# Two-layer hybrid trunk on one core: homes for a layer's first weights, order of the end-of-layer squares, stream order of the last product, queue of the solve's loads

## The chip, the cores and the metric

The kernel runs on one core of one Trainium2 chip. The core's engines work from queues of their own and meet through semaphores: TensorE (PE; its weight loads PEld), VectorE (DVE), ScalarE (ACT), GpSimd (POOL) and SyncE (SP), and DMA queues that ACT, POOL and SP issue. The metric is the device time of one execution in microseconds (us); lower is better.

## The reference, cut to what matters

```python
for l in range(2):                                  # DEPTH; x is (1, 256, 2048), float32
    h = rmsnorm(x, norm_pre[l])                     # x * rsqrt(mean(x*x) + 1e-6) * gain
    pa, pb, pc, pd, pm = split(h @ w_in[l])         # four mixers' columns and the merge gates
    ys = [gla(pa), sparse_attention(pb), rwkv7(pc), spatial_gating(pd)]   # each (256, 1024)
    merged = sum(sigmoid(pm[g]) * (ys[g] @ w_proj[l, g]) for g in range(4))
    x = x + rmsnorm(merged @ w_out[l], norm_post[l])
```

The rwkv7 mixer is a recurrence in time; the kernel computes it in chunks, for which small triangular systems are solved. All matrix products are to be right to float32.

## The kernel before, in words

**Weights as one stream.** The 256 tokens are two halves of 128, t = 0 and 1. All large weights lie in one DRAM tensor `w`, packed by the host in the order in which they are used. `weights()` (L187) reads it on SyncE's queue: one DMA brings four k-steps (128 rows of the contraction each) into a `raw` tile, 1 MB where a product is 512 wide; there are three such tiles (RAW_BUFS = 3). Each k-step is split into a high part `wh` (ACT, L154) and a rest `wl` (DVE, L157), and six matmuls follow, three for each half of the tokens (`tok_mm`, L169). `wh` and `wl` have three buffers each, so the splits run at most three k-steps ahead of TensorE. Steps named in `apart` get tiles of their own (`wown`), which wait for none of the three; for steps named in `alone`, the three matmuls of t = 0 come first, and those of t = 1 only after the last such step.

**Order.** The framework lays the program out on a timeline that it works out when the kernel is built, with priorities; after that each engine executes its own list in that fixed order. A wait on an engine holds all that stands behind it in the list.

**A layer.** `pre` transposes the normalised tokens (`trT`, L173) and evicts each block twice: a high part on ACT, the rest on DVE (`xT`). `small` (L455) is the first product, 280 wide, with nine steps in `wown`, in tiles of class `c8`. Eight products `c_pair` follow (tile `mc` on TensorE), then `c_solve` (L628), then the other mixers, the merges and `finish`.

**The solve.** During the c_pairs, POOL writes factors to DRAM (`Gd`). `c_solve` reads them back in another layout: eight loads of 64 KB into `slv` (L637) and four into `TT` (L657), all issued by ACT's queue, while TensorE runs the next product. DVE then works through the substitution (`slvt`, `slv`).

**The end of a layer.** `finish` (L1010) runs four products d = 0..3 with `w_out`. For each and each half, ACT squares the result (`junk`, with a sum) and DVE scales it into `o`. The last, d = 3, keeps steps 8..15 in `wown` (also class `c8`, four buffers) and has 5..15 in `alone`: t = 0 is complete before t = 1's long stretch. Then come the sum of squares (`orsq`, whose power is on POOL), `x <- o*orsq + x` (L1040) in four quarters per half, the write of x to DRAM (`xs`, L1041, POOL's queue) and, in layer 0, the norm of the next layer: four Squares on ACT, the sum and power (`ss`, POOL L183), and the scaled result, again in `o`, two quarters on DVE and two on ACT. At the start of the program the norm of each half takes two quarters by `bn_stats` on DVE and two by Squares on ACT.

Of the kernel before, what the change touches and what calls it, by code (L numbers as in the profile page):

```python
# [30 lines left out]
RAW_BUFS, SPLIT_BUFS = 3, 3  # L31

# [46 lines left out]
def pack_stream(w_in, w_proj, w_out, depth=DEPTH):  # L79
    parts = []  # L80
    for l in range(depth):
        for kind, g, cols in blocks():
# [4 lines left out]
            parts.append(s.reshape(k // rk, rk, 128, n).transpose(0, 2, 1, 3).reshape(-1))  # L87
# [41 lines left out]
class Trunk:  # L129
# [56 lines left out]
    def weights(self, nk, width, apart=(), shift=0):  # L186


        n = 2048 // (2 * width)
        m = 0  # L190
# [3 lines left out]
        for q in range(nk // rk):  # L194
# [4 lines left out]
            for b in range(rk):  # L199
                if q * rk + b in apart:  # L200
                    if m % n == 0:
                        own = self.t("c8", [128, n, 2, width], "wown", F32R)
                    wh, wl = own[:, m % n, 0, :], own[:, m % n, 1, :]
                    m += 1
# [7 lines left out]
    def product(self, xT, nk, width, apart=(), alone=()):  # L212


        pa = [self.ps.tile([128, width], F32, name=f"mm{t}", tag="mm", bufs=4) for t in range(2)]
        held = []
        for k, wh, wl in self.weights(nk, width, apart):
            if k in alone:
                with self.tc.high_priority():
                    self.tok_mm(pa, xT[k], wh, wl, k == 0, k == nk - 1, (0,))  # L220
                held.append((k, wh, wl))
                if k + 1 not in alone:
                    for k, wh, wl in held:
                        self.tok_mm(pa, xT[k], wh, wl, k == 0, k == nk - 1, (1,))
            else:
                self.tok_mm(pa, xT[k], wh, wl, k == 0, k == nk - 1)
        return pa
# [141 lines left out]
    def norm(self, x, h, stats=False):  # L369

        s1 = self.one([128, 1], "ss1", bufs=2)
        ss = self.one([128, 4], "ss", bufs=2)
        for c in range(2 if stats else 4):
            junk = self.t("t2", [128, 512], "junk")
            self.act(junk, x[:, c * 512:(c + 1) * 512], AF.Square, accum_out=ss[:, c:c + 1])
        if stats:
            st, mv = self.t("c1", [128, 2, 6], "nst"), self.t("s1", [128, 2], "nmv")
            for c in range(2):
                self.nc.vector.bn_stats(st[:, c, :], x[:, (c + 2) * 512:(c + 3) * 512])
            self.nc.vector.bn_aggr(mv, st.rearrange("p b s -> p (b s)"))  # L380
            self.stt(ss[:, 2:3], mv[:, 0:1], mv[:, 0:1], mv[:, 1:2], OP.mult, OP.add)
            self.stt(s1, ss[:, 2:3], 1024.0, ss[:, 0:1], OP.mult, OP.add)
# [706 lines left out]
```

## Time and profile before

| | us |
|---|---|
| median of 3 runs (2810.72 to 2812.64) | 2812.59 |
| the profiled execution, whole | 2813.03 |
| its span in the trace | 2811.2 |
| TensorE busy in the span | 2773.3 (99%) |
| DVE, ACT, POOL busy | 1813.3 (65%), 1484.9 (53%), 176.2 (6%) |
| TensorE waiting for `trT` <- `x`, at the start | 11.2 |
| TensorE waiting for `trT` <- `o`, between the layers | 7.1 |
| TensorE waiting for `mm` <- `wh`, 4 times | 3.0 |

The times are of the slowest core, here the only one. The span runs from the first to the last recorded event; 1.83 us of the profiled execution lie outside it. Overlapping matmuls make a busy share of 99%; a pause of TensorE shows as a wait or as a step that takes longer than its neighbours. The row of a timeline gives start, duration, engine, line, operation, output <- input and count, and in square brackets the engine's idle time before it and what ended that.

### The profile page before, as it was taken

What the parts mean: (1) busy time and instruction counts of PE and PEld (TensorE: products, weight loads), DVE (VectorE), ACT (ScalarE), POOL (GpSimd) and SP (SyncE); (2) the same over time, 40 slices, a digit from 0 to 9 for tenths busy, and PEclk for the clock granted to TensorE, in tenths of its full rate; (3) what the DMA queues carried; (4) which work ended last, traced back from release to release, by engine and by line L of the source; (5) the groups of instructions that cost most, each with busy time, mean ns of one, the idle gap of its engine ahead of it and who ended that gap; (6) DMA issues with size and microseconds to landing.
All of it is one profiled execution on the core that took longest, in us unless ns stands there. A gap on an engine that the chain in (4) does not pass through costs nothing. (4 is left out here: it accounts for less than half of the span.)

```text
span 2811.2 us, 44812 instructions
## 1 busy us (share of the span) xinstructions
PE 2773.3 (99%) x17264; PEld 2411.8 (86%) x17264; DVE 1813.3 (65%) x3269; ACT 1484.9 (53%) x2639; POOL 176.2 (6%) x254
## 2 busy tenths in 40 slices
PE   8999999999999999999999999999999999999998
PEld 7998889888788898888789988898887889988886
DVE  7777957555555655556577778675555556655565
ACT  6554555555554455445565556555555544544554
POOL 1222011000000000000012210100000000000000
PEclk9999999999999999999999999999999999999999
DMA  5555545554455555555555564455555555555554
GB/s 207 191 188 189 186 166 197 182 201 174 172 200 192 207 203 193 196 188 186 182 196 183 197 205 171 162 199 185 188 180 179 195 195 196 209 192 193 192 187 157
DMA packets 92478, 531.45 MB, mean 189 GB/s; under 512 B 22532, under 2 KB 22788, under 8 KB 32678
## 3 DMA queue, kind: packets, MB, share of 16 engines
q1 hardware_dynamic: 68256, 486.96, 49.7%
q10 hardware_dynamic: 18248, 22.75, 2.5%
q0 software_dynamic: 5760, 18.88, 2.1%
q8 instruction: 135, 2.21, 0.3%
q14 instruction: 79, 0.65, 0.1%
HBM read 511.78 MB, written 16.78 MB: 188 GB/s over the span
## 5 line engine op out<-in xcount | busy, mean ns | idle before, releaser
L157 DVE TENSOR_TENSOR wl<-raw,wh 128x512 fp32r<-128x512 f32 (+1 forms) x1822 | 1248.9, 689 | 893.3 <-ACT wh L154 882.9
L154 ACT ACTIVATE wh<-raw 128x512 fp32r<-128x512 f32 (+1 forms) x1822 | 1145.4, 630 | 1139.6 <-DVE wl L157 635.6
L169 PE MATMUL mm<-wh,xT 128*128 128x512 f32 (+1 forms) x4216 | 1315.3, 390 | 3.0 <-ACT wh L154 3.0
L169 PEld LDWEIGHTS mm<-wh,xT 128*128 128x128 f32 x4216 | 786.7, 188 | 170.2 <-ACT wh L154 10.4
L169 PE MATMUL mm<-wl,xT 128*128 128x512 f32 (+1 forms) x2108 | 828.3, 393 | 0.8 <-DVE wl L157 0.6
L169 PE MATMUL mc<-xT,wh 128*128 128x256 f32 x3072 | 529.5, 282 | 0.0
L169 PEld LDWEIGHTS mm<-wl,xT 128*128 128x128 f32 x2108 | 395.8, 188 | 88.0 <-DVE wl L157 5.4
L169 PEld LDWEIGHTS mc<-xT,wh 128*128 128x128 f32 x3072 | 447.5, 189 | 1.5
L169 PE MATMUL mc<-xT,wl 128*128 128x256 f32 x1536 | 380.9, 283 | 3.3 <-DVE wl L157 3.0
L169 PE MATMUL mm<-wh,yT 128*128 128x512 f32 x1024 | 321.0, 389 | 0.0
L169 PEld LDWEIGHTS mc<-xT,wl 128*128 128x128 f32 x1536 | 266.2, 189 | 6.6 <-DVE wl L157 5.6
L169 PEld LDWEIGHTS mm<-wh,yT 128*128 128x128 f32 x1024 | 192.1, 188 | 41.2 <-ACT aex L154 1.5
L169 PE MATMUL mm<-wl,yT 128*128 128x512 f32 x512 | 199.4, 389 | 0.0
L169 PE MATMUL mb<-wh,xT 128*128 128x256 f32 x512 | 117.6, 283 | 0.0
L169 PEld LDWEIGHTS mm<-wl,yT 128*128 128x128 f32 x512 | 96.1, 188 | 19.9
L169 PE MATMUL mb<-xT,wh 128*128 128x256 f32 x512 | 101.9, 282 | 0.0
L169 PEld LDWEIGHTS mb<-wh,xT 128*128 128x128 f32 x512 | 87.4, 188 | 2.0 <-issue 0.8
L169 PEld LDWEIGHTS mb<-xT,wh 128*128 128x128 f32 x512 | 78.6, 188 | 0.9 <-issue 0.5
L169 PE MATMUL mb<-wl,xT 128*128 128x256 f32 x256 | 74.5, 291 | 0.0
L169 PE MATMUL mb<-xT,wl 128*128 128x256 f32 x256 | 72.3, 282 | 0.0
L183 POOL TENSOR_TENSOR orsq<-orsq,mhalf 128x1 f32<-128x1 f32 x4 | 2.3, 585 | 884.8 <-DVE orsq L163 884.8
L169 PEld LDWEIGHTS mb<-wl,xT 128*128 128x128 f32 x256 | 48.2, 188 | 1.6 <-DVE slv L157 0.5
(290 smaller groups left out, 1843.9 us busy)
## 6 DMA issues: line engine op xcount, KB each, us to landing
raw<-in_w_dram SPq DMA_DIRECT2D x456, 1024.0 KB, 4.8
Gd<-G POOLq DMA_DIRECT2D x32, 256.0 KB, 3.1
Gq<-Gd ACTq DMA_DIRECT2D x8, 1024.0 KB, 5.9
raw<-in_w_dram SPq DMA_DIRECT2D x8, 560.0 KB, 4.3
bsd<-bs POOLq DMA_DIRECT2D x16, 256.0 KB, 4.2
bs<-bsd POOLq DMA_DIRECT2D x16, 256.0 KB, 3.1
x<-in_x_dram ACTq DMA_DIRECT2D x4, 512.0 KB, 5.0
x<-in_x_dram SPq DMA_DIRECT2D x4, 512.0 KB, 6.9
```

The costliest lines, as they stand in the source:

```text
L154: self.nc.scalar.activation(out, in_, f, **kw)
L157: (eng or self.nc.vector).tensor_tensor(out, a, b, op)
L169: self.nc.tensor.matmul(out, lhsT, rhs, start=start, stop=stop, **kw)
L183: self.nc.gpsimd.tensor_tensor(out, out, self.mhalf[:, :n], OP.pow)
```

## The change

Five edits, all within `weights`, `product`, `norm`, `small`, `c_solve`, `finish` and the host's packing.

1. `small` keeps eight steps instead of nine, in tiles of classes `tt` (three steps), `ev` (two) and `zz` (three) instead of `c8`. The memsets of the zero-padded `zz` tiles (`wbd`, `sbd`, POOL), once ahead of the first weights, now follow `small`.
2. The last product's weights come in another order: k = 8..11, 12..15, 0..3, 4..7 (LATE). The matmuls keep their order.
3. At the end of a layer all of d = 3's Squares and the norm's write one `junk` tile, which puts them in a fixed order, and the update of x and the norm of t = 0 stand ahead of t = 1's square, at high priority.
4. The first norm takes t = 0 by `bn_stats` alone and scales it on DVE alone; t = 1's sums are all Squares on ACT.
5. The eight `slv` and four `TT` loads go to SyncE's queue, behind and ahead of the weights there.

```diff
+LATE = (2, 3, 0, 1)
@@ pack_stream: s is (k/4, 4, 128, n)
+            if kind == "out" and cols[0][1] == DM:
+                s = s[list(LATE)]
@@ def weights(self, nk, width, apart=(), shift=0, homes=None, order=None):
-        for q in range(nk // rk):
+        homes = homes or [("c8", 2048 // (2 * width))] * 4
+        for q in order or range(nk // rk):
...
-                    if m % n == 0:
-                        own = self.t("c8", [128, n, 2, width], "wown", F32R)
+                    if not free:
+                        cls, n = homes[0]
+                        homes = homes[1:]
+                        own = self.t(cls, [128, n, 2, width], "wown", F32R)
+                        free = [own[:, m] for m in range(n)]
@@ def product(...): with an order, the kept steps are sorted by k, all of t = 0 first
+        if order:
+            held.sort(key=lambda s: s[0])
+            half(held, 0)
+            half(held, 1)
@@ def norm(self, x, h, stats=False, junk=None):
-        for c in range(2 if stats else 4):
-            junk = self.t("t2", [128, 512], "junk")
-            self.act(junk, x[:, c * 512:(c + 1) * 512], AF.Square, accum_out=ss[:, c:c + 1])
         if stats:
-            for c in range(2):
-                self.nc.vector.bn_stats(st[:, c, :], x[:, (c + 2) * 512:(c + 3) * 512])
+            for c in range(4):
+                self.nc.vector.bn_stats(st[:, c, :], x[:, c * 512:(c + 1) * 512])
...
+            for c in range(4):
+                z = self.t("t2", [128, 512], "junk") if junk is None else junk
+                self.act(z, x[:, c * 512:(c + 1) * 512], AF.Square, accum_out=ss[:, c:c + 1])
...
-            if c % 2:
+            if c % 2 and not stats:
@@ def small(self):
-        pa = self.product(self.xT, KT, 280, range(9), range(9))
+        pa = self.product(self.xT, KT, 280, range(8), range(8), [("tt", 3), ("ev", 1), ("ev", 1), ("zz", 1), ("zz", 1), ("zz", 1)])
@@ c_solve: eight loads into M (slv), and four into TT alike
-                    nc.scalar.dma_start(M[g:g + 16], Gd[...])
+                    nc.sync.dma_start(M[g:g + 16], Gd[...])
@@ def finish(self, src, last):
-            pa = self.product(self.mT, KT, 512, *((range(8, KT), range(5, KT)) if d == 3 else ()))
+            pa = self.product(self.mT, KT, 512, *((range(8, KT), range(5, KT), None, LATE) if d == 3 else ()))
+            junk = self.t("t2", [128, 512], "junk") if d == 3 else None
             for t in range(2):
...
+                for c in range(4):
+                    s = slice(c * 512, (c + 1) * 512)
                     with self.tc.high_priority():
+                        self.stt(X[t][:, s], o[t][:, c], s1[t], X[t][:, s], OP.mult, OP.add)
+                    (nc.gpsimd if not last else nc.sync if c % 2 else nc.scalar).dma_start(dst[t, :, s], X[t][:, s])
+                if not last:
+                    with self.tc.high_priority():
+                        self.norm(X[t], o[t], junk=junk)
@@ run: the first norm
-                self.norm(X[t], H[t], True)
+                self.norm(X[t], H[t], t == 0)
```

**ACT, from the product d = 2 into d = 3 of layer 0.** A number in a name is a tile of its own; `raw_13932` before and `raw_13930` after hold d = 2's steps 12..15. Before, with `raw_13982` for d = 3's steps 0..3, `raw_14057` for its 8..11 and `raw_14024` for its 4..7:

```order
L154 ACTIVATE wh_13954<-raw_13932 128x512 [waits DVE_49,PE_49]
L154 ACTIVATE wh_13964<-raw_13932 128x512 [waits DVE_49,PE_49]
L154 ACTIVATE wh_13984<-raw_13982 128x512 [waits DMAHW2_49,DVE_49,PE_49]
L154 ACTIVATE wh_13994<-raw_13982 128x512 [waits DVE_49,PE_49]
L154 ACTIVATE junk_13974,osum0_13449<-mm0_13804 128x512 [waits PE_49]
L154 ACTIVATE wh_14004<-raw_13982 128x512 [waits DVE_49,PE_49]
L154 ACTIVATE junk_13977,osum1_13450<-mm1_13805 128x512
L154 ACTIVATE wh_14014<-raw_13982 128x512 [waits DVE_49,PE_49]
L154 ACTIVATE wown_14059<-raw_14057 128x512 [waits DMAHW4_49]
L154 ACTIVATE wown_14059<-raw_14057 128x512
L154 ACTIVATE wown_14070<-raw_14057 128x512 x2
L154 ACTIVATE wh_14026<-raw_14024 128x512 [waits DMAHW3_49,DVE_49,PE_49]
```

After, with `raw_13980` for d = 3's steps 8..11, `raw_13992` for 12..15 and `raw_14004` for 0..3:

```order
L158 ACTIVATE wh_13920<-raw_13888 128x512 [waits DVE_49,PE_49]
L158 ACTIVATE wown_13982<-raw_13980 128x512 [waits DMAHW2_49]
L158 ACTIVATE wown_13982<-raw_13980 128x512
L158 ACTIVATE wown_13987<-raw_13980 128x512 x2
L158 ACTIVATE wh_13932<-raw_13930 128x512 [waits DMAHW1_49,DVE_49,PE_49]
L158 ACTIVATE wh_13942<-raw_13930 128x512 [waits DVE_49,PE_49]
L158 ACTIVATE wh_13952<-raw_13930 128x512 [waits DVE_49,PE_49]
L158 ACTIVATE wown_13994<-raw_13992 128x512 [waits DMAHW3_49]
L158 ACTIVATE wown_13994<-raw_13992 128x512
L158 ACTIVATE wown_13999<-raw_13992 128x512 x2
L158 ACTIVATE wh_13962<-raw_13930 128x512 [waits DVE_49,PE_49]
L158 ACTIVATE wh_14006<-raw_14004 128x512 [waits DMAHW4_49,DVE_49,PE_49]
```

The eight kept splits of d = 3 moved from behind d = 3's first four steps to between d = 2's last five; two of them wait for a DMA there.

**DVE, between the layers.** `o_13451`/`o_13448` with input `mm1` scales d = 3 of t = 1; the TENSOR_REDUCE rows sum the squares (`ss1`: the norm of t = 0); `x0`, `x1` are the updates; `o <- x0, ss1` is what the next layer transposes. Before:

```order
L157 TENSOR_TENSOR wown_14351<-raw_14339,wown_14351 128x280 [waits Activation_49]
L1034 TENSOR_REDUCE orsq_14148<-osum1_13450 128x1 [waits Activation_49]
L157 TENSOR_TENSOR o_13451<-mm1_13981,npost_13447 128x512
L163 TENSOR_SCALAR orsq_14148<-orsq_14148 128x1 [waits DVE_49]
L385 TENSOR_REDUCE ss1_14161<-ss_14162 128x1 [waits Activation_49]
L163 TENSOR_SCALAR ss1_14161<-ss1_14161 128x1 [waits DVE_49]
L166 SCALAR_TENSOR_TENSOR x1_13442<-o_13451,orsq_14148,x1_13442 128x512 [waits Pool_49]
L166 SCALAR_TENSOR_TENSOR x1_13442<-o_13451,orsq_14148,x1_13442 128x512 x3
L161 TENSOR_SCALAR o_13451<-x0_13439,ss1_14161 128x512 [waits Pool_49]
L161 TENSOR_SCALAR o_13451<-x0_13439,ss1_14161 128x512
```

After:

```order
L170 SCALAR_TENSOR_TENSOR x0_13436<-o_13448,orsq_14139,x0_13436 128x512 [waits DVE_49]
L400 TENSOR_REDUCE ss1_14151<-ss_14152 128x1 [waits Activation_49]
L167 TENSOR_SCALAR ss1_14151<-ss1_14151 128x1 [waits DVE_49]
L1053 TENSOR_REDUCE orsq_14166<-osum1_13447 128x1 [waits Activation_49]
L161 TENSOR_TENSOR o_13448<-mm1_13979,npost_13444 128x512
L167 TENSOR_SCALAR orsq_14166<-orsq_14166 128x1 [waits DVE_49]
L165 TENSOR_SCALAR o_13448<-x0_13436,ss1_14151 128x512 [waits Pool_49]
L165 TENSOR_SCALAR o_13448<-x0_13436,ss1_14151 128x512
L170 SCALAR_TENSOR_TENSOR x1_13439<-o_13448,orsq_14166,x1_13439 128x512 [waits Pool_49]
L170 SCALAR_TENSOR_TENSOR x1_13439<-o_13448,orsq_14166,x1_13439 128x512 x2
L170 SCALAR_TENSOR_TENSOR x1_13439<-o_13448,orsq_14166,x1_13439 128x512 [waits DVE_49]
L170 SCALAR_TENSOR_TENSOR xT_14193<-trT_14197,pcol_14191,xT_14193 128x128 [waits Activation_49]
```

The norm of t = 0 moved ahead of all that hangs on t = 1's square, its result ahead of t = 1's four updates, and these now stand directly ahead of the first `xT` eviction.

**The solve's loads, layer 0.** Before, ACT's list (`raw_4392` holds steps 4..7 of the product that runs then):

```order
L154 ACTIVATE wh_4394<-raw_4392 128x512 [waits DMAHW3_49,DVE_49,PE_49]
L637 DMA slv_3316<-Gd_474 16x32x32 [waits DMASW5_49,DMASW3_49,DMASW6_49,DMASW2_49,DMASW0_49]
L154 ACTIVATE wh_4404<-raw_4392 128x512 [waits DVE_49,PE_49]
L637 DMA slv_3316<-Gd_474 16x32x32 x4
L154 ACTIVATE wh_4414<-raw_4392 128x512 [waits DVE_49,PE_49]
L637 DMA slv_3316<-Gd_474 16x32x32
L637 DMA slv_3316<-Gd_474 16x32x32 [waits DMAHW4_49]
L637 DMA slv_3316<-Gd_474 16x32x32 [waits DMAHW5_49]
L154 ACTIVATE wh_4424<-raw_4392 128x512 [waits DVE_49,PE_49]
```

After, SP's list:

```order
L200 DMA raw_4473<-in_w_dram 128x2048 [waits DMAHW2_49,DVE_49]
L652 DMA slv_3313<-Gd_471 16x32x32 [waits DMASW4_49,DMASW3_49,DMASW5_49,DMASW2_49,DMASW6_49,DMASW1_49,DMASW7_49,DMASW0_49,PE_49]
L652 DMA slv_3313<-Gd_471 16x32x32 x4
L652 DMA slv_3313<-Gd_471 16x32x32 [waits DMAHW3_49]
L652 DMA slv_3313<-Gd_471 16x32x32 [waits DMAHW4_49]
L652 DMA slv_3313<-Gd_471 16x32x32 [waits DMAHW5_49]
L672 DMA TT_3387<-Gd_471 32x16x32 [waits DMAHW6_49,PE_49]
L672 DMA TT_3387<-Gd_471 32x16x32 [waits DMAHW0_49]
L672 DMA TT_3387<-Gd_471 32x16x32 [waits DMAHW1_49]
L672 DMA TT_3387<-Gd_471 32x16x32 [waits DMAHW2_49]
L200 DMA raw_4541<-in_w_dram 128x2048 [waits DMAHW3_49,DVE_49]
```

And DVE's list after, at the same place (`raw_4431` holds steps 8..11; `bias` belongs to the sparse attention):

```order
L161 TENSOR_TENSOR wl_4434<-raw_4431,wh_4433 128x512 [waits DMAHW4_49,Activation_49]
L170 SCALAR_TENSOR_TENSOR bias_4244<-rl_4253,iw_460,bias_4244 128x128 [waits DVE_49,Activation_49]
L161 TENSOR_TENSOR slvt_3324<-slv_3313 128x31 [waits DMAHW3_49,DMAHW4_49,DMAHW2_49,DMAHW5_49,DMAHW1_49,DMAHW6_49,DMAHW0_49,DMAHW7_49,DMASW4_49,DMASW3_49]
L170 SCALAR_TENSOR_TENSOR bias_4244<-rl_4253,iw_460,bias_4244 128x128 [waits DVE_49]
L161 TENSOR_TENSOR slv_3313<-slv_3313,slvt_3324 128x31 [waits DVE_49]
L161 TENSOR_TENSOR slvt_3324<-slv_3313 128x2x30 [waits DVE_49]
L161 TENSOR_TENSOR wl_4444<-raw_4431,wh_4443 128x512 [waits Activation_49]
```

The loads left ACT's list, where splits stood between and behind them; the first `slvt`, which waits for all eight, stands between the splits of steps 8 and 9 in DVE's.

## Rows read from the trace of the kernel before

**Rows 1.** The page, busy time by engine; then its costliest group on DVE.
```profile
PE 2773.3 (99%) x17264; PEld 2411.8 (86%) x17264; DVE 1813.3 (65%) x3269; ACT 1484.9 (53%) x2639; POOL 176.2 (6%) x254
...
L157 DVE TENSOR_TENSOR wl<-raw,wh 128x512 fp32r<-128x512 f32 (+1 forms) x1822 | 1248.9, 689 | 893.3 <-ACT wh L154 882.9
```
**Rows 2.** Timeline of the boundary between the layers: ACT's rows.
```profile
1405.43 0.60 ACT L154 ACTIVATE junk<-mm 128x512 f32<-128x512 f32 x1 [0.27 <-PE mm L169]
...
1406.01 0.62 ACT L154 ACTIVATE junk<-x 128x512 f32<-128x512 f32 x1
...
1409.78 1.34 ACT L154 ACTIVATE o<-x,ss 128x512 f32<-128x512 f32 x2 [1.22 <-POOL ss L183]
```
**Rows 3.** The same timeline, DVE's rows.
```profile
1401.87 1.42 DVE L166 SCALAR_TENSOR_TENSOR x<-o,orsq,x 128x512 f32<-128x512 f32 x2 [0.44 <-POOL orsq L183]
...
1409.26 2.74 DVE L166 SCALAR_TENSOR_TENSOR x<-o,orsq,x 128x512 f32<-128x512 f32 x4 [0.32 <-POOL orsq L183]
1411.91 0.88 DVE L161 TENSOR_SCALAR o<-x,ss 128x512 f32<-128x512 f32 x2
...
1414.64 0.35 DVE L166 SCALAR_TENSOR_TENSOR xT<-trT,pcol,xT 128x128 fp32r<-128x128 f32 x1 [0.70 <-ACT xT L154]
```
**Rows 4.** The same timeline, PE's rows.
```profile
1399.79 5.60 PE L169 MATMUL mm<-wown,xT 128*128 128x512 f32 x24
...
1412.45 3.67 PE L173 MATMUL trT<-cst,o 128*128 128x128 f32 x16 [7.06 <-DVE o L161]
...
1431.05 0.63 PE L169 MATMUL mc<-xT,wh 128*128 128x256 f32 x4
```
**Rows 5.** Stretches there: length, busy time and count per engine, granted clock, DMA share, GB/s.
```profile
1408.00:1414.00 6.00, 1.55 (x8) 1.55 (x9) 4.73 (x12) 4.35 (x12) 3.47 (x7) 0.50 0.99 332
...
1416.00:1418.00 2.00, 2.00 (x12) 2.00 (x12) 1.49 (x7) 1.84 (x8) 0.00 (x0) 0.60 1.02 369
```
**Rows 6.** DMAs of the writes of x (xs) there, from issue to landing.
```profile
DMA to landing us min/median/max: 2.7/6.1/10.0
```
**Rows 7.** Timeline of the start, rows of DVE, POOL and PE.
```profile
5.63 1.29 DVE L379 BATCH_NORM_STATS2 nst<-x 128x6 f32<-128x512 f32 x2 [5.63 <-DMA x<-in_x_dram]
...
10.61 1.84 DVE L161 TENSOR_SCALAR x<-x,ss 128x512 f32<-128x512 f32 x4
...
9.81 0.57 POOL L183 TENSOR_TENSOR ss<-ss,mhalf 128x1 f32<-128x1 f32 x1 [0.67 <-DVE ss L163]
...
11.16 3.67 PE L173 MATMUL trT<-cst,x 128*128 128x128 f32 x16 [11.16 <-DVE x L161]
```
**Rows 8.** Timeline of the solve in layer 0, rows of ACT's queue, DVE and PE.
```profile
274.83 4.39 ACTq L637 DMA_DIRECT2D slv<-Gd  x4
...
283.29 0.19 DVE L157 TENSOR_TENSOR slvt<-slv 128x31 f32<-128x31 f32 x1
...
278.40 0.39 PE L169 MATMUL mm<-wh,xT 128*128 128x512 f32 x1
...
284.53 0.84 PE L169 MATMUL mm<-wh,xT 128*128 128x512 f32 x3
```
**Rows 9.** Timeline of the solve in layer 1, PE.
```profile
1674.87 0.39 PE L169 MATMUL mm<-wh,xT 128*128 128x512 f32 x1
...
1680.55 0.85 PE L169 MATMUL mm<-wh,xT 128*128 128x512 f32 x3
```
**Rows 10.** Timeline from product d = 2 into d = 3: ACT and PE of layer 0, PE of layer 1.
```profile
1380.48 0.63 ACT L154 ACTIVATE wh<-raw 128x512 fp32r<-128x512 f32 x1 [0.73 <-DVE wl L157]
...
1389.49 2.19 ACT L154 ACTIVATE wown<-raw 128x512 fp32r<-128x512 f32 x4 [1.57 <-DMA raw<-in_w_dram]
...
1381.41 0.84 PE L169 MATMUL mm<-wh,xT 128*128 128x512 f32 x3
...
2784.76 0.73 PE L169 MATMUL mm<-wh,xT 128*128 128x512 f32 x2 [0.56 <-ACT wh L154]
```
**Rows 11.** The weights' DMAs of 2770 to 2790 us, issue to landing.
```profile
DMA to landing us min/median/max: 4.8/5.0/5.9
```

## What the change will do to the time

> **What bounds the kernel now.** I read the page first: TensorE is busy 2773.3 of 2811.2 us [rows 1], so a change can win only where TensorE pauses or where a step of six matmuls takes longer than its usual 1.36 us. That usual step is ACT's rhythm in the last product: 0.63 us for a split and 0.73 of waiting [rows 10]. Then I read the list of waits, and the timelines of the four places that the edits touch: the start, the solve in each layer, the run from product d = 2 into d = 3 in each layer, and the boundary between the layers. The profiled execution took 2813.03 us, 1.83 more than its span; the sum is made against it, and the median of the runs, 2812.59, is 0.44 lower.
>
> **The boundary (edits 1 and 3).** Call A the end of t = 0's long stretch and B that of t = 1's. The second stretch of 24 kept matmuls runs from 1399.79 to 1405.39 [rows 4], so A is about 1399.5, B is 1405.39, and 5.9 us lie between. Between A and B nothing that t = 0 needs waits for t = 1. Yet before, ACT's and DVE's lists hold `small`'s kept splits there, which wait for the `c8` tiles that TensorE frees as it goes (edit 1 takes them away); the Square of t = 1 at 1405.43 comes ahead of x0's four, which begin at 1406.01, and the scaled result follows at 1409.78 on ACT and 1411.91 on DVE, there behind x1's updates of 2.74 us [rows 2, 3]. TensorE resumes at 1412.45, after 7.06 us [rows 4].
>
> Now the replay with the new order. x0's first update starts at A+2.4, as before (1401.87 [rows 3]); four without splits between them take 2.74 [rows 3], to A+5.1. Each Square follows its update, the last until A+5.85 (they overlap to about 0.52 each). Sum, scale and power take 1.22 (ACT's idle time before 1409.78 [rows 2]): A+7.1. DVE is then scaling t = 1's product until A+7.4, and a quarter of `o` (0.88 for two [rows 3]) is ready at A+7.9. TensorE pauses 7.9 - 5.9 = 2.0 us in place of 7.06: 5.1 less.
>
> What is late next: x1's four updates, 2.74 us, ran before the transposes and now stand between DVE's second quarter and its first `xT` rest. They end at A+11.0, the first rest at A+11.4, that is 3.5 after the transposes began, against 2.2 before (1414.64 [rows 3]). TensorE can't start `small` until it has the rests, so about 0.9 comes back. From the transposes to the first `mc` it was 1431.05 - 1412.45 = 18.6 us [rows 4]; I put it at 19.5, so `mc` starts at A+27.4 in place of A+31.55. The granted clock was 0.50 in 1408 to 1414, the lower level of 1.2 GHz, and still 0.60 in 1416 to 1418 [rows 5]: the pause took the clock with it, and the first six us of work paid. With a pause of 2.0 and thin work after it the low clock may come again or last longer; I take 0.7 off, with 0 and 2.5 as bounds (in the 6 us at 0.50 TensorE was busy 1.55 [rows 5], and two like stretches follow). **The boundary gains 3.5, from 1.5 to 6.5.**
>
> The first edit's price: the memsets of the `zz` tiles move from idle POOL time at the start to behind `small`. They are first used in `c_chain`, behind all c_pairs, and POOL is busy in 6% of the span [rows 1]: its idle time hides them, and I cost them at nothing. Were it gone, each would hold POOL's list, the c_pairs' small powers included, for its length.
>
> **From d = 2 into d = 3 (edit 2).** Before, d = 3 starts at 1381.64 (one matmul of 0.23 after 1381.41 [rows 10]) and ends at 1405.39; 96 matmuls at 0.227 (24 in 5.60, less the drain of 0.16 [rows 4]) are 21.8, and with the drain that leaves 1.8 lost, where the kept splits waited for their DMA (ACT 1.57 at 1389.49) and held the next splits. Layer 1 shows the like (0.56 at 2784.76 [rows 10]); I take the same 1.8. After, the kept raws come first, and their eight splits (0.55 each on ACT, so 4.4) stand between d = 2's last five. The spare time of a step is 0.73, so three steps and the lead of the three buffers don't hold 4.4. Worked through with a landing of 4.85 (4.8 to 5.9 [rows 11]): d = 2's step 12 is late by 0.25, step 15 by 1.4, 1.64 in all; after that d = 3's splits keep ahead to the end. **So 1.64 replaces 1.8: 0.3 gained in two layers.** The new wait is the DMA's on ACT in the middle of d = 2; behind it stand d = 2's own splits, and behind them TensorE. A landing of 5.9 at both kept raws costs up to 1 us for each: the bounds are a loss of 3 and a gain of 1.5.
>
> **The start (edit 4).** All of t = 0's sums on DVE: from 5.63, four `bn_stats` at 0.645 [rows 7] end at 8.2, the small steps at 8.85, the power (0.57) at 9.45, where it was 10.4. But DVE then scales all four quarters at 0.46, and the second transpose in TensorE's list reads the third quarter, ready at 10.9. The row of transposes began at 11.16 [rows 7]; I put it 0.3 earlier, and the evictions behind it 0.5 earlier in all. ACT's two more Squares of t = 1 (1.0) lie ahead of its first weights' splits: **0.5 gained, from a loss of 1 to a gain of 1.5.**
>
> **The solve (edit 5).** Before, ACT's queue spends 4.39 us on four loads [rows 8], and the splits behind them wait. TensorE's three steps from 278.40 to 284.53 [rows 8] take 6.13 in place of 4.08, and from 1674.87 to 1680.55 [rows 9] 5.68: 2.05 + 1.60 = 3.65 lost. After, ACT is free. But the first `slvt`, which waits for all eight loads, now stands ahead of step 9's split on DVE. In layer 0, undisturbed, step 9 would want that rest at 278.63 + 3 x 1.36 + 0.45 = 283.2. It is ready 0.9 (two `slvt`, `slv`, a `bias`) and 0.69 [rows 1] after the last load has landed, so TensorE waits as long as the landing is past 281.6. Before, all eight had landed by 283.29 [rows 8]; if SyncE issues at the same pace, I reckon with 282 to 283.2, a wait of 0.4 to 1.6. I take 1.0 in each layer: **3.65 - 2.0 = 1.6 gained, from a loss of 0.5 to a gain of 3.65.** Behind the loads on SyncE's queue stand the weights of the following product. They would go out near 283.5 and land near 288.3 (4.8 [rows 11]); their splits are wanted seven steps after step 9's start of 282.7, near 292: hidden.
>
> The row that decides is the 4.39: were it ACT's own doing, SyncE would issue faster and land earlier. The Trainium skill, "Trainium Kernel Development and Optimization", Key Constraints, speaks against a gain in landing: loads issued from SyncE, ACT and POOL run on the same DMA engines, and issuing from several saves only issue time. By that rule the loads land as late as before, the wait on DVE is the full 1.6 and the term is 0.4 in place of 1.6, the time 2808; by the rows' best case (landing by 281.6) it is 3.65.
>
> **The sum.** 3.5 + 0.3 + 0.5 + 1.6 = 5.9. From 2813.03 that is 2807.1, and from the median 2806.7, my forecast. 0.2% of the median, about what a measurement of this kernel can tell from no change, is 5.6 us, so the line for faster is 2807.0: the forecast lies on it.
>
> **Rivals.**
> (a) *The boundary's wait is only replaced.* In ACT's new list the load of `w2` waits until the four writes of x0 have landed, and all high parts of `xT` stand behind it. Issued at A+3.5 to A+5.8 and landing in 2.7 to 4.2, x0's are in by A+10, hidden behind x1's updates. But the eight writes took 2.7 to 10.0 [rows 6], with the DMA share at 0.99 just then [rows 5]. From A+10 on each us late costs one; four eat the term. The sum falls to 2.4: 2810.2. For it: the busy DMAs; against: it was x1's writes that took 8 to 10.
> (b) *Slower: late weights in d = 2's tail.* The two waits on ACT pass a late landing on to TensorE, at steps 12 and 15 of both layers. At 7.7 in place of 4.85 each wait grows by 2.85, 11.4 in all, and the sum of 5.9 becomes a loss of 5.5: 2818. It is slower than before from a landing of about 6.3 on. Against it: 4.8 to 5.9 is all that this place showed [rows 11].
> (c) *The solve's stall only moves* from ACT to DVE: 1.6 goes, 2808.3.
> (d) *The boundary is covered better.* If the evictions keep up and the clock stays at 2.4 GHz, 96 matmuls of `small` at 280/512 of 0.227, 0.124, and 32 transposes at as much (an estimate) are 15.9 after the transposes begin, not 19.5; with no clock loss the term is 5.1 + 18.6 - 15.9 = 7.8 in place of 3.5: 2802.4. The Trainium skill, "TensorE: Matmul & The Clock Gate", Part 1, says that "the default state is throttled, and activity releases the throttle". By that, thin work after the pause would not release it, which is (a)'s side; rows 5 agree, with 0.50 while little ran.
>
> **How the numbers follow.** The forecast gets 0.44, (a) 0.22, (c) 0.13, (d) 0.15, (b) 0.06. The bounds of the four terms do not all fall on one side at once; taken as independent they give 3.9 below and 4.6 above. With (d) and (a) this makes 2801.5 to 2811.5, which leaves out half of (b) and the tails, under 2 in 10. Faster by over 0.2%: (d) and more than half of the forecast, with little of (c): 0.47. Within 0.2%: the rest of it, (a) and (c): 0.47. Slower: 0.06.
>
> **What would show it.** The wait of `trT` for `o` near 2 us in place of 7.06, and 25.7 us from B to the first `mc` becoming about 21.5; x0's Squares on ACT ahead of t = 1's; ACT waiting for `raw` between d = 2's steps 11 and 15, and d = 3 without a wait; no gap on ACT at the solve and a wait of DVE's `slvt` for `slv`. I am wrong if the clock between the layers stays low beyond six us after the transposes begin, if ACT idles at `w2`, if the kept weights land past 6 us, or if the solve's steps are as long as before.

## The result, and the profile after

The changed kernel takes 2850.31 us (median of 4 runs, 2848.28 to 2851.43) against 2811.65 (2810.31 to 2812.64): a ratio of 1.0134 with a 95% interval of 1.0122 to 1.0146. It is 38.7 us slower, where 2806.7 was forecast and 2811.5 was the upper end of the range.

First the page of the kernel after: span, busy time by engine, and the costliest groups (out<-in, count, busy and mean ns of one, idle before).

```profile
span 2849.4 us, 44812 instructions
...
PE 2815.0 (99%) x17264; PEld 2426.9 (85%) x17264; DVE 1813.4 (64%) x3266; ACT 1484.9 (52%) x2637; POOL 178.0 (6%) x254
...
L161 DVE TENSOR_TENSOR wl<-raw,wh 128x512 fp32r<-128x512 f32 (+1 forms) x1824 | 1249.1, 689 | 908.0 <-ACT wh L158 900.4
...
L173 PE MATMUL mm<-wh,xT 128*128 128x512 f32 (+1 forms) x4224 | 1333.9, 394 | 1.4 <-ACT wh L158 1.4
...
L173 PE MATMUL mm<-wl,xT 128*128 128x512 f32 (+1 forms) x2112 | 836.4, 396 | 2.9 <-DVE wl L161 2.9
...
L173 PE MATMUL mm<-wh,yT 128*128 128x512 f32 x1024 | 327.0, 395 | 0.0
...
L173 PE MATMUL mm<-wl,yT 128*128 128x512 f32 x512 | 202.6, 396 | 0.0
...
L173 PE MATMUL mc<-xT,wh 128*128 128x256 f32 x3072 | 539.4, 284 | 0.0
```

The same matmul groups on the page of the kernel before, which the rows ahead of the prediction don't have:

```profile
L169 PE MATMUL mm<-wh,xT 128*128 128x512 f32 (+1 forms) x4216 | 1315.3, 390 | 3.0 <-ACT wh L154 3.0
...
L169 PE MATMUL mm<-wl,xT 128*128 128x512 f32 (+1 forms) x2108 | 828.3, 393 | 0.8 <-DVE wl L157 0.6
...
L169 PE MATMUL mm<-wh,yT 128*128 128x512 f32 x1024 | 321.0, 389 | 0.0
...
L169 PE MATMUL mm<-wl,yT 128*128 128x512 f32 x512 | 199.4, 389 | 0.0
...
L169 PE MATMUL mc<-xT,wh 128*128 128x256 f32 x3072 | 529.5, 282 | 0.0
```

TensorE is busy 41.7 us more than in [rows 1] with the same 17264 matmuls, and idle 3.5 us less (2849.4 - 2815.0 = 34.4, against 2811.2 - 2773.3 = 37.9). So the pauses shrank, and the work itself became longer. DVE and ACT are as busy as before, and one `wl` takes 689 ns in both. The mean long matmul is 3 to 7 ns longer, group by group. Busy times of neighbouring matmuls overlap, so the groups' gains can't be added up; taken from one start to the next in the two traces, with gaps over 0.6 us left out, the `mm` take 29.8 us more (19.8 with `xT`, 10.0 with `yT`) and the 256-column `mc` 12.6 (565.8 against 553.2). The granted clock is no cause: its mean is 0.997 after and 0.996 before.

The step of six matmuls shows it without any modelled end, from one start to the next. Timeline of the kernel after, deep inside a product that reads `yT` (start, length, engine, line, tiles, count, idle before):

```profile
1130.74 0.86 PE L173 MATMUL mm<-wh,yT 128*128 128x512 f32 x3
...
1132.14 0.86 PE L173 MATMUL mm<-wh,yT 128*128 128x512 f32 x3
...
1131.17 0.63 ACT L158 ACTIVATE wh<-raw 128x512 fp32r<-128x512 f32 x1 [0.77 <-PE mm L173]
```

The kernel before at the same time, where a product with `xT` runs (its products with `yT` have the same step):

```profile
1130.23 0.84 PE L169 MATMUL mm<-wh,xT 128*128 128x512 f32 x3
...
1131.59 0.84 PE L169 MATMUL mm<-wh,xT 128*128 128x512 f32 x3
...
1130.65 0.63 ACT L154 ACTIVATE wh<-raw 128x512 fp32r<-128x512 f32 x1 [0.73 <-DVE wl L157]
```

A step was 1.36 us (0.2267 for a matmul) and is 1.40 here (0.2333); over whole products of the kernel after it is 0.229 to 0.233 for a matmul. ACT's split is 0.63 as before and only waits longer, now for TensorE.

Two of the four places that the prediction replayed, in the timeline of the kernel after (PE at the boundary, with the last 24 kept matmuls of d = 3, then DVE and PE at layer 0's solve):

```profile
1422.06 5.76 PE L173 MATMUL mm<-wown,xT 128*128 128x512 f32 x24
1430.56 3.15 PE L177 MATMUL trT<-cst,o 128*128 128x128 f32 x16 [2.73 <-DVE o L165]
...
1450.42 0.63 PE L173 MATMUL mc<-xT,wh 128*128 128x256 f32 x4
...
289.96 0.19 DVE L161 TENSOR_TENSOR slvt<-slv 128x31 f32<-128x31 f32 x1 [3.66 <-DMA TT<-Gd]
...
291.42 0.80 PE L173 MATMUL mm<-wl,xT 128*128 128x512 f32 x1 [2.55 <-DVE wl L161]
```

The pause between the layers is 2.73 in place of the 7.06 of [rows 4]. At the solve TensorE waits 2.55 for a `wl` that stands behind the first `slvt` on DVE.

### The profile page after: what moved, and what is told of

The parts are those of the page before. It is cut to its first block, busy times and chain, and to the rows that moved or that the text cites. A ratio compares the mean times of both kernels' runs of the same rounds, so it can differ in the third digit from the quotient of the medians.

```text
span 2849.4 us, 44812 instructions
## 1 busy us (share of the span) xinstructions
PE 2815.0 (99%) x17264; PEld 2426.9 (85%) x17264; DVE 1813.4 (64%) x3266; ACT 1484.9 (52%) x2637; POOL 178.0 (6%) x254
## 5 line engine op out<-in xcount | busy, mean ns | idle before, releaser
L173 PE MATMUL mm<-wh,xT 128*128 128x512 f32 (+1 forms) x4224 | 1333.9, 394 | 1.4 <-ACT wh L158 1.4
L173 PE MATMUL mc<-xT,wh 128*128 128x256 f32 x3072 | 539.4, 284 | 0.0
L173 PE MATMUL mm<-wh,yT 128*128 128x512 f32 x1024 | 327.0, 395 | 0.0
L173 PEld LDWEIGHTS mb<-xT,wl 128*128 128x128 f32 x256 | 48.2, 188 | 0.1
```

Source lines behind the costliest of these rows:

```text
L173: self.nc.tensor.matmul(out, lhsT, rhs, start=start, stop=stop, **kw)
```

## Why every matmul became longer

**The suspicion.** The instructions on TensorE are the same, so I looked at where their operands lie in SBUF. Tile classes get their places in the order of their first use in the program. Before, `small`'s kept steps use `c8` first; with edit 1 they use `tt`, `ev` and `zz`, and `c8` comes later. By the addresses in the built programs `wh`, `wl` and `yT` (a `c8` tile) move with it. The table gives the place of each tile's start modulo 256 bytes, in twelve kernels (`wl` is as `wh` where one number stands). In a matmul of `mm`, `wh` or `wl` streams and `xT` or `yT` is the loaded, stationary side; the distance is that between the two places. In `mc` the weights are the stationary side and `xT` streams, and there the source starts the weights 64 bytes into their tile (`shift=16`), so that the distance of `mc` is 64 before and 128 after.

| kernel | xT | yT | wh, wl | ratio to before |
|---|---|---|---|---|
| before | 32 | 32 | 32 | 1 |
| after | 32 | 160 | 96 | 1.0134 |
| before_homes | 32 | 160 | 96 | 1.0142 |
| before_shift | 32 | 32 | 96 | 1.0113 |
| after_align | 32 | 32 | 160 | 1.0159 |
| after_256 | 32 | 32 | 32 | 1.0000 |
| before_xT64 | 96 | 32 | 32 | 1.0188 |
| before_wl64 | 32 | 32 | wh 32, wl 96 | 1.0172 |
| b_off32 | 32 | 32 | 64 | 1.019 (one run) |
| b_off224 | 32 | 32 | 0 | 1.019 (one run) |
| b_all64 | 96 | 96 | 96 | 0.9986 |
| b_all224 | 0 | 0 | 0 | 0.9993 |

The shifts are made with a helper that asks the pool for a tile that nobody uses:

```diff
+    def pad(self, name, nbytes):
+        if name not in self.pads:
+            self.pads.append(name)
+            self.sb.tile([128, nbytes // 4], F32, name=name, tag=name, bufs=1)
```

It changes no instruction and no order: on every engine the list is that of the kernel it was made from.

**before_shift and after_align**: 64 bytes of nothing ahead of `wh` and behind `wl`, in the kernel before and in the kernel after.

```diff
+        self.pad("pad0")             # 64 bytes each in these two runs
         wh, wl = ...
+        self.pad("pad1")
```

> The kernel before, with every instruction in its old place in every engine's order; only wh and wl lie 64 bytes further on each partition (wh from 142880 to 142944), and what lies behind them 128 bytes further. Theory 'place': the long matmuls run at 0.229 to 0.233 us in place of 0.227 because of where the split tiles came to lie in memory; then this kernel alone is slower by 30 to 45 us (2843 to 2857), with the same pitch of 0.229 to 0.233 in its products. Theory 'order': the pitch comes from the new order of instructions or from the loads on SyncE's queue; then 2811 to 2813, pitch 0.227.

> The changed kernel, with every instruction in its place in every engine's order; only wh and wl lie 64 bytes further (wh from 138848 to 138912), which puts them at the same offset within 128 bytes as in the kernel before, and what lies behind them 128 bytes further. Theory 'place': the pitch is 0.227 again and the time is what the prediction summed, 2802 to 2811. Theory 'order': 2848 to 2852, as the changed kernel. If the place matters but not by 64 bytes (the distance to other tiles, say), it stays near 2850 too, and before_shift tells the two apart.

Measured: before_shift 2843.61, ratio 1.0113 (1.0099 to 1.0126); after_align 2857.09, 1.0159 (1.0145 to 1.0173). So a shift of `wh` and `wl` by 64 bytes slows the old kernel by 31 us, with nothing else of the change in it: layout alone can do it. Its page:

```profile
PE 2806.0 (99%) x17264; PEld 2427.3 (85%) x17264; DVE 1812.6 (64%) x3269; ACT 1485.2 (52%) x2639; POOL 175.4 (6%) x254
...
L176 PE MATMUL mm<-wh,xT 128*128 128x512 f32 (+1 forms) x4216 | 1327.2, 393 | 2.1 <-ACT wh L161 2.1
```

But after_align, which restored the offset modulo 128, didn't mend the kernel after; with 160 against 32 it was worse, and slower than either theory had it. My first theory, that a tile's place modulo 128 is what counts, fell.

**before_homes and before_solve**: the kernel before with edit 1 alone (the lines of `weights` and `product` that take the new argument are left out), and with edit 5 alone (the four `TT` loads go the same way).

```diff
-        pa = self.product(self.xT, KT, 280, range(9), range(9))
+        pa = self.product(self.xT, KT, 280, range(8), range(8), [("tt", 3), ("ev", 1), ("ev", 1), ("zz", 1), ("zz", 1), ("zz", 1)])
```

```diff
-                    nc.scalar.dma_start(M[g:g + 16], Gd[...])
+                    nc.sync.dma_start(M[g:g + 16], Gd[...])
```

> The kernel before with edit 1 alone: small keeps eight steps, in tiles of classes tt, ev and zz. This edit alone moves the split tiles (wh to 138848, as in the changed kernel). Theory 'place': 2835 to 2855, pitch 0.229 to 0.233. Theory 'order': the pitch stays 0.227 and the boundary gets shorter or stays: 2805 to 2813.

> The kernel before with edit 5 alone: the solve's loads on SyncE's queue; all tiles stay where they were. Theory 'place': pitch 0.227 everywhere, and the prediction's term of the solve, a gain of 1.6 (from a loss of 0.5 to a gain of 3.65): 2809 to 2813. Theory 'order', if the loads on SyncE are what slows the matmuls: 30 us or more slower.

Measured: before_homes 2852.42, 1.0142 (1.0128 to 1.0156), the whole loss. before_solve 2815.82 (2811.82 to 2818.99), 1.0011 (1.0002 to 1.0020): a small loss, above the 2809 to 2813 expected, taken up below.

**after_256 and before_raw64**: the kernel after with 192 bytes ahead of `wh` and 192 behind `wl`, which puts all operands of TensorE back to 32 modulo 256; and the kernel before with `raw`, which TensorE doesn't read, moved by 64 alone.

```diff
+        self.pad("pad0", 192)
         wh, wl = ...
+        self.pad("pad1", 192)
```

> The changed kernel with every instruction in its old place in the order; wh and wl 192 bytes further (wh from 138848 to 139040), the tiles behind them 384 further. In the kernel before, raw, xT, yT, wh and wl all begin at 32 within 256 bytes; in before_shift and in the changed kernel wh and wl stood at 96 (64 off the others), in after_align at 160 (128 off). Here all begin at 32 again. Theory 'offset within 256': pitch of the long matmuls 0.227 again, and the time is what the five edits are worth without the shift, 2800 to 2812. Theory 'distance or another period': 2840 to 2860 as in the three shifted kernels.

> The kernel before, same order, raw alone 64 bytes further (85600); all behind it 256 further, so that their offsets within 256 stay. Theory 'TensorE's own two reads' (the moving tile wh or wl against the stationary tile xT or yT): nothing changes, 2811 to 2814, pitch 0.227. Theory 'ACT and DVE beside TensorE' (they read raw while they write wh and wl, and TensorE suffers from where these streams meet): slower by 15 us or more.

Measured: after_256 2812.81, ratio 1.0000 (0.9991 to 1.0009); before_raw64 2811.86, 1.0000 (0.9991 to 1.0009). The page of after_256:

```profile
PE 2776.1 (99%) x17264; PEld 2412.3 (86%) x17264; DVE 1814.2 (64%) x3266; ACT 1484.3 (53%) x2637; POOL 176.6 (6%) x254
...
L180 PE MATMUL mm<-wh,xT 128*128 128x512 f32 (+1 forms) x4224 | 1321.2, 390 | 1.5 <-ACT wh L165 1.5
```

384 bytes of nothing take the loss away: 390 ns for a `wh` matmul, as before. Where `raw` lies, which ACT and DVE read, plays no part.

**before_xT64 and before_wl64**: in the kernel before `xT` alone moved by 64, and `wl` alone.

```diff
+        self.pad("padx0", 64)
         self.xT = ...
+        self.pad("padx1", 192)
```

```diff
         wh = ...
+        self.pad("pad0", 64)
         wl = ...
+        self.pad("pad1", 192)
```

> The kernel before, same order, xT alone 64 bytes further (52832); all behind it 256 further. Theory 'TensorE's own two reads': the products with xT (most of them) run at 0.229 to 0.233, those with yT stay at 0.227; 2835 to 2850. Theory 'ACT and DVE beside TensorE': pitch 0.227, 2811 to 2814.

> The kernel before, same order, wl alone 64 bytes further (149856), wh where it was, all behind 256 further. Theory 'TensorE's own two reads': one matmul of three has a shifted moving tile, so a third of before_shift's loss of 31 us: 2820 to 2825, the matmuls on wl longer and those on wh not. Theory 'ACT and DVE beside TensorE': the loss is spread over all matmuls whatever they read, of any size up to 31.

Measured: 2864.50, 1.0188 (1.0174 to 1.0202), and 2860.47, 1.0172 (1.0157 to 1.0188). Both lost more than expected. before_xT64 is the cleanest test, since in one program `xT` lies apart from the weights of `mm` and `yT` doesn't. Page and timeline of before_xT64:

```profile
L176 PE MATMUL mm<-wh,xT 128*128 128x512 f32 (+1 forms) x4216 | 1337.3, 395 | 2.2 <-ACT wh L161 2.1
...
L176 PE MATMUL mm<-wh,yT 128*128 128x512 f32 x1024 | 321.4, 390 | 0.0
...
L176 PE MATMUL mm<-wl,yT 128*128 128x512 f32 x512 | 199.7, 390 | 0.0
...
L176 PE MATMUL mc<-xT,wh 128*128 128x256 f32 x3072 | 543.2, 285 | 0.0
...
1131.96 0.84 PE L176 MATMUL mm<-wh,yT 128*128 128x512 f32 x3
...
1133.32 0.84 PE L176 MATMUL mm<-wh,yT 128*128 128x512 f32 x3
...
1138.83 0.86 PE L176 MATMUL mm<-wh,xT 128*128 128x512 f32 x3
...
1140.23 0.86 PE L176 MATMUL mm<-wh,xT 128*128 128x512 f32 x3
```

With `yT` a step takes 1.36, and seven us later with `xT`, from the same buffers of weights, 1.40. So the weights' place by itself isn't the cause, nor a stage of the program: it is how the tiles lie to each other. For `mc` another distance is the good one: in before_xT64 its two tiles are the ones at distance 0, and it is slowest there, 569.4 us from start to start, against 553.2 before (the weights 64 past `xT`), 565.8 in the kernel after (128) and 562.4 in after_align (64 the other way). before_wl64 was a miss in kind as well as in size. I had expected only the matmuls of `wl`, a third, to become longer; all did, those of `wh` too, which had kept their place:

```profile
L176 PE MATMUL mm<-wh,xT 128*128 128x512 f32 (+1 forms) x4216 | 1336.9, 395 | 2.2 <-ACT wh L161 2.2
...
L176 PE MATMUL mm<-wl,xT 128*128 128x512 f32 (+1 forms) x2108 | 838.8, 398 | 0.6 <-DVE wl L164 0.6
```

So the two tiles of one matmul are not all that counts: where the tiles of the matmuls beside it lie counts too.

**b_off32, b_off224, b_all64 and b_all224**: the kernel before with `wh` and `wl` moved by 32 and by 224; and with `xT` and all behind it moved together, by 64 and by 224.

```diff
+        self.pad("pad0", 32)         # b_off224: 224
         wh, wl = ...
+        self.pad("pad1", 224)        # b_off224: 32
```

```diff
+        self.pad("padx0", 64)        # b_all224: 224
         self.xT = ...
```

> The kernel before, same order, wh and wl 32 bytes further (64 within 256, the others at 32), all behind them 256 further. A look at how the pitch depends on the distance: 0 gave 0.227, 64 and 128 and -64 gave 0.229 to 0.235. Theory 'every distance costs': 2825 to 2865. Theory 'it is the 64-byte piece that counts': 32 and 64 lie in different pieces, so it costs as 64 does, about 2843; that the 0.227 can be beaten: below 2800.

> The kernel before, same order, wh and wl 224 bytes further (0 within 256, the others at 32: 32 before them), all behind them 256 further. Theory 'every distance costs': 2825 to 2865. Theory 'it is the 64-byte piece that counts': 0 and 32 lie in the same piece, 2811 to 2814.

> The kernel before, same order, with xT and everything behind it (raw, yT, wown, wh, wl and the rest) 64 bytes further: all of TensorE's tiles begin at 96 within 256, their distances stay 0. Theory 'the distance counts': 2811 to 2814, pitch 0.227. Theory 'each tile must begin at 32': 2840 to 2870.

> The same with 224 bytes: all of TensorE's tiles begin at 0 within 256, distances 0. Theory 'the distance counts': 2811 to 2814, pitch 0.227. If a start at a round multiple of 256 is better still, under 2800; if it is a bad place, 2840 to 2870.

Measured: 2866.46 and 2865.65 for a distance of 32 either way (one run each, beside 2812.86 for before); 2807.85, 0.9986 (0.9974 to 0.9997), and 2809.10, 0.9993 (0.9982 to 1.0004), where all moved together. The page of b_off32, with the last 24 kept matmuls of d = 3 from its timeline, then the page of b_all64:

```profile
L176 PE MATMUL mm<-wh,xT 128*128 128x512 f32 (+1 forms) x4216 | 1338.0, 395 | 2.3 <-ACT wh L161 2.3
...
1427.18 5.62 PE L176 MATMUL mm<-wown,xT 128*128 128x512 f32 x24
```

```profile
L176 PE MATMUL mm<-wh,xT 128*128 128x512 f32 (+1 forms) x4216 | 1315.5, 390 | 2.5 <-ACT wh L161 2.5
```

A theory of 64-byte pieces (a shift inside one piece costs nothing) fell with b_off224, where 0 and 32 lie in one piece; both times are just above the 2825 to 2865 of the theory that every distance costs. The kept tiles `wown` check it within one program: in b_off32 they lie at 32 as `xT` does, and their 24 matmuls take 5.62 us, as before (5.60 [rows 4]), while every step from `wh` and `wl` is longer; in the kernel after, where `wown` lies at 160, they take 5.76. What is left fits all twelve kernels, for the 512-column `mm`: a step of six is 1.36 us where all its streamed and stationary tiles lie at distance 0 modulo 256, whatever the place (0, 32 or 96), and 1.37 to 1.40 where one of them lies at any other distance tried: 32, 64, 128 and back by 32 or 64.

## What the five edits do with the layout put right

**a_1234 and a_123**: after_256 without edit 5 (the `TT` loads alike), and without edits 4 and 5 (of edit 4 the call is shown; the sums in `norm` are those of before too).

```diff
-                    nc.sync.dma_start(M[g:g + 16], Gd[...])
+                    nc.scalar.dma_start(M[g:g + 16], Gd[...])
```

```diff
-                self.norm(X[t], H[t], t == 0)
+                self.norm(X[t], H[t], True)
```

> after_256 (the changed kernel with the split tiles at 32 within 256 bytes) without edit 5: the solve's loads go out on ACT's queue again. In after_256's trace DVE's slvt waits 3.66 us for the loads, TensorE 2.62, and the clock falls to 0.50 for 3.4 us behind it; the solve of layer 0 ends 3.8 later than before. Theory 'the solve edit eats what the boundary gains': 2807 to 2810, faster than after_256 by 2 to 5. Theory 'the boundary gains nothing in the timed runs': 2811 to 2814.

> a_1234 without edit 4 as well: the first norm of each half again two quarters on DVE and two on ACT. In after_256's trace the transposes begin 0.50 earlier than before, but the first c_pair 0.59 later. Theory 'edit 4 costs about 1 there': 0.5 to 1.5 faster than a_1234. Theory 'edit 1 costs it (eight kept steps in place of nine)': the same as a_1234.

Measured: a_1234 2810.59, 0.9992 (0.9983 to 1.0001); a_123 2809.99, 0.9988 (0.9979 to 0.9997). With after_256 at 1.0000, taking edit 5 away gains about 0.08%, 2.3 us, and taking edit 4 away some 0.04%. The intervals overlap, so these runs can't tell either from nothing; for edit 5 the loss of before_solve points the same way. a_123 is faster than both kernels, than the kernel before by 2.9 us.

**The boundary**, in the timeline of after_256 (ACT, then DVE and PE):

```profile
1407.57 0.63 ACT L165 ACTIVATE junk<-x 128x512 f32<-128x512 f32 x1 [2.16 <-DVE x L177]
...
1410.40 0.63 ACT L165 ACTIVATE junk<-x 128x512 f32<-128x512 f32 x1
...
1412.18 1.34 ACT L165 ACTIVATE o<-x,ss 128x512 f32<-128x512 f32 x2 [0.34 <-POOL ss L194]
...
1406.73 2.74 DVE L177 SCALAR_TENSOR_TENSOR x<-o,orsq,x 128x512 f32<-128x512 f32 x4 [0.44 <-POOL orsq L194]
...
1413.14 3.53 PE L184 MATMUL trT<-cst,o 128*128 128x128 f32 x16 [2.90 <-DVE o L172]
...
1433.06 0.63 PE L180 MATMUL mc<-xT,wh 128*128 128x256 f32 x4
```

The updates run as replayed, in one piece of 2.74. The pause is 2.90, and from the transposes to the first `mc` it is 19.92. B to `mc` is 22.8 us in place of 25.66: 2.85 gained.

**The solve of layer 0**, in the timeline of after_256 (queues of SP and ACT, then ACT, DVE and PE), and two stretches of its granted clock (length, busy and count of PE, PEld, DVE, ACT and POOL, clock, DMA share, GB/s):

```profile
275.29 5.92 SPq L661 DMA_DIRECT2D slv<-Gd  x8
...
281.10 0.36 ACTq L716 DMA_DIRECT2D Gq<-Gd  x1
...
281.51 0.38 ACT L165 ACTIVATE rl<-psc 128x256 f32<-128x256 f32 x1 [2.56 <-DMA slv<-Gd]
...
287.13 0.19 DVE L168 TENSOR_TENSOR slvt<-slv 128x31 f32<-128x31 f32 x1 [3.66 <-DMA TT<-Gd]
...
288.60 0.50 PE L180 MATMUL mm<-wl,xT 128*128 128x512 f32 x1 [2.62 <-DVE wl L168]
...
284.00:288.00 4.00, 1.98 (x9) 1.32 (x7) 0.83 (x5) 1.22 (x3) 0.00 (x0) 1.00 1.27 256
288.00:292.00 4.00, 3.40 (x9) 2.04 (x10) 3.93 (x14) 0.63 (x1) 0.00 (x0) 0.75 0.60 233
```

And in the timelines of before_solve and of a_1234, at the same place:

```profile
284.06 0.19 DVE L157 TENSOR_TENSOR slvt<-slv 128x31 f32<-128x31 f32 x1 [0.73 <-DMA slv<-Gd]
```

```profile
280.22 0.73 PE L180 MATMUL mm<-wh,xT 128*128 128x512 f32 x2 [0.70 <-ACT wh L165]
...
283.50 0.18 DVE L168 TENSOR_TENSOR slvt<-slv 128x31 f32<-128x31 f32 x1
```

From the matmuls of `piq` to the first `mb` the solve of layer 0 takes 24.68 us before, 28.47 in after_256 and 24.15 in a_1234, of which layer 1 shows little (24.26, 24.23, 24.50). The eight loads go out on SP at the pace they had on ACT, 275.3 to 281.2. Two things follow. `Gq`, a load on ACT's queue that waits for other loads, now keeps ACT from 279 to 281.5: the [2.56] of `rl`. And DVE waits at `slvt` for the loads, to 284.06 in before_solve, where TensorE does not pause for it (23.91 us from `piq` to `mb`), but to 287.13 in after_256. There TensorE pauses 2.62, and the granted clock falls to the lower level, 1.2 GHz, for part of the next stretch (0.75 in the mean). In these two traces edit 5 gains 0.8 or costs 3.8 us in layer 0, by when the loads come in. The 11 times of before_solve spread over 7.2 us (2811.82 to 2818.99), those of a_1234 over 3.4; that the landings make this spread is not shown, with one trace of each.

What came late in after_256 is not the loads as a whole. The trace counts each load's landing in 16 parts: of the eighth load, 14 parts had landed by 283.22, and the last two came at 284.75 and 286.81. In the kernel after 15 had landed by 286.05 and the last came at 289.64; in before_solve all were in by 283.74.

## Why the prediction was wrong

**The step that failed is the first edit's price.** The prediction put it at the `zz` memsets on POOL, hidden in idle time, and wrote "I cost them at nothing". For POOL that fits, 178.0 us busy against 176.2. But the edit cost 40 us in before_homes through the places of `wh`, `wl` and `yT`. All four terms of the sum, and all four rivals, took the step of 1.36 us as given. The prediction called that step ACT's rhythm, but it is TensorE's own spacing: as the matmuls became longer, ACT's split stayed at 0.63 us and its wait grew. The rival on the slower side (b) was about late weights in d = 2's tail and is not what happened: there the waits stayed small (below). Nothing in the rows ahead of the prediction showed what a distance costs, since in the kernel before all `mm` are at distance 0 and all `mc` and `mb` at 64; the addresses could have been read from the built programs, though, and were not, and the `shift=16` in the source shows that a place had been set by hand.

**The other terms**, read in after_256 against before, where the layout is put right:

| term | foretold (bounds) | traces |
|---|---|---|
| boundary | 3.5 (1.5 to 6.5) | 2.85 |
| d = 2 into d = 3 | 0.3 (-3 to 1.5) | -0.2 |
| start, to the first `mc` | 0.5 (-1 to 1.5) | -0.6 |
| solve | 1.6 (-0.5 to 3.65) | -3.8 |
| sum | 5.9 | -1.8 |

The sum fits the profiled execution's span of 2812.9, 1.7 over 2811.2 before. Each figure is read from one execution of each kernel, and the like stretch can differ by 1 us between executions (see the start), so the two small terms say no more than that they are small.

- *Boundary*: the mechanism was right and the size a little off. The pause was 2.9 for 2.0: the four Squares, each with its 0.19 us read of the accumulator, ended at 1411.1, 0.9 later than reckoned from the overlap of two. The way from the transposes to `mc` was 19.9 for 19.5. The granted clock of 0.50 came again, for about 3.4 us in place of 10.2, and ACT did not idle at `w2`, so neither (a) nor (d) came about.
- *d = 2 into d = 3*: right in kind and size. In after_256 d = 3 took 22.9 and 21.9 us in place of 23.75 and 23.69, and d = 2's tail was late by nearly as much; over both, layer 0 lost 0.62 and layer 1 gained 0.40. In a_1234 both gained, 0.22 and 0.33.
- *Start*: the transposes began 0.5 earlier (10.66), as reckoned, but the first `mc` came at 35.74 for 35.16. The term stopped at the evictions and left out what comes behind them. What edit 4 costs is not settled: a_123, without it, has its first `mc` at 34.27 and a_1234, with it, at 35.46, but the kernel after, with it too, at 34.45, and before and before_shift, both without it and alike up to there but for the places, at 35.16 and 34.10.
- *Solve*: the sign was wrong, in after_256's trace and in before_solve's median, through the landing. I took 282 to 283.2 in layer 0; the loads were in at 283.7 in before_solve and 286.8 in after_256, beyond the bounds. In before_solve's own trace the two solves took 23.91 and 23.94, together 1.1 less than before, so with a landing near 283.7 the foretold sign can come out. And `Gq`'s wait on ACT, ahead of the splits, was not in the replay, though the order of ACT's list shows it. What the Trainium skill says in "Trainium Kernel Development and Optimization", Key Constraints, that issuing from several engines saves issue time alone, agrees with the loads' pace (5.9 us on SP, and on ACT 274.38 to 280.84), and 2808, worked out by it, was still too kind: no row of before told how much later than 283.2 the last part of a load can land.

Without the layout's part, then, where 5.9 was forecast, the medians gain nothing with all five edits, 2.3 with edits 1 to 4 (not clear of noise) and 2.9 with edits 1 to 3. Of the rivals, (c), the solve's stall that only moves, names what happened there, though not its size.

**What stays open.** Why a step at a distance is sometimes 1.37 and sometimes 1.40 us is not settled: in before_shift most products run at 0.229 for a matmul and one stretch of each layer at 0.2333, with the same tiles. Nor is it shown why the matmuls of `wh` become longer when `wl` alone moves, why `mc` is fastest with its weights 64 past `xT`, nor why the last parts of one of the solve's loads land at 283.7 in one kernel and 286.8 in another.

## What to carry to other kernels

An edit that changes which tile class is used first moves every tile behind it: compare the addresses of TensorE's operands in the built programs before and after, and put their distances back, if need be by a few hundred bytes of padding. Here the 512-column products ran fastest with all their tiles at one place modulo 256 bytes, the 256-column `mc` with the weights 64 past `xT`, so the good distance is to be measured for each shape. When the busy time of the bound engine changes with the same instructions, look at the starts of like instructions in a steady stretch before any queue or wait. And when loads are moved to another queue, what pays or costs is who waits for their landing in list order, which one profiled execution shows at one landing time only.

## What the hardware showed that I had not expected

At the full granted clock, 2.4 GHz, the spacing of 512-column matmuls depends on where two tiles lie to each other: 0.2267 us at distance 0 modulo 256 bytes, 0.229 to 0.234 at 32, 64 or 128, with none of the engine's waits in the profile showing it. Over this kernel, the 256-column products included, a shift costs 31 to 54 us, 1.1 to 1.9%.

The Trainium skill, "SBUF — State Buffer", Who interferes with whom, gives TensorE two read ports, one for the streamed side and one for loading weights, calls them independent, and says that "PE and ACT never wait on anyone". On other engines the runs show nothing against it: where `raw` lies, which ACT and DVE read, changes nothing in before_raw64 (ratio 1.0000). But if independent means that neither side's time depends on the other, the measurements differ, with 1.36 us for a step in before_xT64 with `yT` and 1.40 with `xT`: whatever the ports do, the time of a matmul here depends on how the streamed and the stationary tiles lie to each other. The runs don't show the mechanism.
